# A two-layer decoder trunk: the sums of the adaLN modulation, from Pool during the attention to VectorE during the input projection

## The chip, the core and the metric

The kernel runs on one core of one Trainium2 chip. The metric is the time of one execution on the device in microseconds, the median over runs. The engines are named as in the profile: PE is TensorE's matmul, PEld its weight load, DVE is VectorE, ACT is ScalarE, POOL is GpSimd ("Pool" here), and SP is the engine that issues most DMAs.

## What is computed

Two layers over 512 tokens of 1024 columns, in float32. Each layer is an attention sub-layer of four groups of heads behind one input projection, and a sub-layer of experts. Both are modulated by six vectors that come from the condition `c`:

```
for l in range(DEPTH):
    mod = jax.nn.silu(c) @ ada_w[l] + ada_b[l]
    sh1, sc1, g1, sh2, sc2, g2 = [m[:, None, :] for m in jnp.split(mod, 6, axis=-1)]
    h = rms_norm(x, norm_mix_g[l]) * (1.0 + sc1) + sh1
    x = x + g1 * hybrid_mixer(h, l, w_in[l], ...)
    h = rms_norm(x, norm_ffn_g[l]) * (1.0 + sc2) + sh2
    x = x + g2 * peer_ffn(h, peer_w_q[l], ...)
```

Each vector is a product of 1024 numbers with a 1024x1024 block of `ada_w`. The change concerns the vectors 2, 3 and 4 of each layer (`g1`, `sh2`, `sc2`). They are not needed before the output projection (`g1`) and the second norm.

## The kernel before

A vector j of the modulation is made in eight steps k. Step k loads 128 rows of its block, 128x1024 or 512 KB, as a tile `aw` (`ada_load`, L223), multiplies every row by its element of silu(c), and adds the result to a sum `aacc`. At the end TensorE adds `aacc` down its 128 partitions (`ada_sum`): for `g1` as a row in two halves (L241), for `sh2` and `sc2` as eight columns (L239). `ada_put` adds the bias; the row of `g1` goes through DRAM (`rowd`) to come back on all partitions (`grow`). The vectors 0 and 1 of layer 0 are made at the start by VectorE with one instruction for a step (`ada_mac`, L218 and L220); vector 5 and the vectors 0 and 1 of layer 1 in the same way during the experts. The vectors 2 to 4 are made during the attention, as below.

The input projection (`w_in_phase`) multiplies the normed rows with `w_in` in seven chunks of 256 to 384 columns. Rows and weights are split in a high and a low part (`hh`, `hl`; `wh`, `wl`), and three matmuls (`mm3`, L203 to L205) make a product. For each chunk four quarters of the weights are loaded (`wr`, two slots), copied by ScalarE to `wh` (L598) and subtracted by VectorE to `wl` (L599); there are six slots of `wh` and `wl`, so the first two quarters of the next chunk can be made early and the other two once the last tile of tokens of this chunk has read its first rows. Then come four tiles of 128 tokens, each with 24 matmuls, whose result VectorE rotates (`rope`, L346 to L348, with its sum on Pool, L349) or ScalarE copies. Behind a chunk stands the making ready of heads (`behind`): Pool or VectorE copies a head twice side by side (`two`, L494), and TensorE transposes it (L497). In layer 0 chunk 0 runs in an order written by hand while the tiles of rows are still normed: `norm_parts` makes `hf` (L318, L320), and `put_split` makes `hh` and `hl` from it (L338, L339). Elsewhere in the projection a scheduler orders the instructions. In layer 1 chunk 0 is done by the end of layer 0.

The attention runs in an order from a planner (`Plan`). Each piece of work has a due time and an engine with a rough length; pieces start when inputs, buffers and engine allow, the most urgent first. Pieces may name several engines. `W` is VectorE working on tiles in SBUF alone and `G` is Pool, and the planner lets both hold a common thing called `port`, so that in its plan they are never at work at once. Its pieces: scores (L851), their maximum (L860), exponentials on ScalarE (L865), the sums' reciprocals, the weights (L874 on ScalarE, L876 on VectorE; for the differential heads L1072, L1077, L1079, L1084), transposes (L884), copies out of PSUM (L790, L792) and sums of values. At the end of the list stands the modulation: loads on SP, a multiplication on Pool or, for each third, on ScalarE (`ada_times`, L273 and L275), and a sum on Pool (L1340), with two buffers `aw` and two `aacc` of the attention's room.

`O`, 128 x 8 x 512, holds the attention's output until the output projection. In layer 0 the input rows lie in it first, a tile of tokens in two of its eight parts; nothing else uses it before the attention.

Of the kernel before, what the change touches and what calls it, by code (L numbers as in the profile page):

```python
# [55 lines left out]
# the chunks of w_in: for each run of columns the size of the rotated heads, the tile, the place in it, the width  # L56
# [7 lines left out]
SV = 0.0  # L64
# [35 lines left out]
class Plan:  # L100
    """an order for pieces of work, from rough lengths: each starts as soon as its inputs, buffers and engine allow, the most urgent first"""
# [28 lines left out]
    def holds(self, eng):  # L130
        """what a piece of work holds: its engine, and the way to SBUF that vector operations on two tiles (W) share with Pool"""
# [20 lines left out]
def trunk(ctx: ExitStack, tc: tile.TileContext, I, out):  # L152
# [81 lines left out]
    def ada_sum(j, acc, c):  # L234
        """sums over the rows, down the partitions or along the free axis"""
# [35 lines left out]
    def ada_times(eng, d, w, k):  # L271
        if eng is S:
            S.activation(d, w, AF.Copy, scale=sil[:, k:k + 1])  # L273
        else:
            eng.tensor_mul(d, w, bc(sil[:, k:k + 1], [128, D]))  # L275

    def norm_cols(l, which):
        """the scale and the shift of a norm, once they are asked for"""
# [13 lines left out]
    def norm_parts(x, cols, pool, put, tag, nv=NV):  # L292
        """normed and modulated rows of one token tile, transposed, four chunks at a time: four steps"""
# [68 lines left out]
    def rows_out(l):  # L362
        """what is done with each tile of rows that leaves layer l - 1"""
        if l == L:
# [19 lines left out]
            def halves(i, x, pool):  # L384
                """the same for a tile of rows that comes in two halves"""
# [28 lines left out]
    def early_mc(nat_):  # L414
        """the place of the first chunk's columns until the tiles they lie in are needed"""
# [3 lines left out]
    def first_chunk(nat_, hh, hl):  # L419
        """the products with the first chunk of w_in, for a tile of rows and some of the inner blocks"""  # L420
# [12 lines left out]
    class Room:  # L433
        """a pool over parts of tiles that nothing else needs yet"""
# [8 lines left out]
    def begin(O, RST, tp, more, hh, hl):  # L443
        """the modulation of the first norm, and what is done around the first chunk of w_in"""
# [39 lines left out]
    def w_in_phase(l, raw_, hh, hl, tp, pa, RST, O):  # L484
        """the products with w_in; what the heads need is made ready behind the chunk that follows"""
# [1659 lines left out]
```

## Time and profile before

| | us |
|---|---|
| three runs | 3385.28, 3389.96, 3396.86 |
| median | 3389.96 |
| span of the profiled execution | 3387.4 |
| median less that span | 2.6 |
| PE, DVE, ACT, POOL busy | 3202.0, 2593.0, 1542.2, 988.0 |

The profile is of one execution, and the page gives its span from the first to the last instruction. The median of the runs is 2.6 us longer, so what is worked out against the span is moved by that much. Layer 0 takes the first half: the projection runs to 161.3, the attention to 334.5, and the output projection and the experts follow; layer 1's projection ends at 1832 and its attention at 2007.3. Busy times overlap: PE's share of 95% of the whole span is a mean over stages, and the attention is one where it is lower.

### The profile page before, as it was taken

The numbers are of one execution on the slowest core, as the hardware profiler recorded it, in microseconds if no ns is written. First come the engines' busy times: TensorE is split into PE (matmuls) and PEld (weight loads), VectorE is DVE, ScalarE is ACT, GpSimd is POOL, SyncE is SP. The second block draws the span as 40 slices with busy tenths as digits, with TensorE's granted clock in tenths as the row PEclk, the third lists the DMA queues.
The fourth block names the chain that finished last, engine by engine and source line by source line (L and its number), as shares of the span: only waits on it lengthen the run. The fifth ranks groups of instructions, "written<-read, shape, count | busy, mean of one in ns | idle before, by whom it ended". The sixth has DMA issues, their size and how long they took to land.

```text
span 3387.4 us, 48323 instructions
## 1 busy us (share of the span) xinstructions
PE 3202.0 (95%) x17540; PEld 2820.4 (83%) x17540; DVE 2593.0 (77%) x5460; ACT 1542.2 (46%) x2799; POOL 988.0 (29%) x756
## 2 busy tenths in 40 slices
PE   6988999979999999999999889999799999999998
PEld 6955879968989999998898568798699899999987
DVE  6487699867878888786665877988587788777766
ACT  3376526883333333333344764278633333333333
POOL 1254120003434343341023532100143344444400
PEclk9988999979999999999998999998799999999999
DMA  6223404458989998896632233044588899999954
GB/s 219 66 92 101 158 26 144 174 210 313 346 308 339 337 335 328 326 351 231 200 117 74 90 125 139 28 154 180 221 320 326 315 341 325 324 324 325 323 186 166
DMA packets 291342, 762.76 MB, mean 225 GB/s; under 512 B 23832, under 2 KB 130968, under 8 KB 285984
## 3 DMA queue, kind: packets, MB, share of 16 engines
q1 hardware_dynamic: 217376, 491.22, 42.0%
q0 software_dynamic: 73728, 268.47, 21.5%
q8 instruction: 137, 2.24, 0.3%
q14 instruction: 101, 0.83, 0.1%
HBM read 700.86 MB, written 58.74 MB: 224 GB/s over the span
## 4 chain that ended last, share of the span: by engine, by line
PE 76%; DVE 13%; ACT 6%; DMA 2%; issue 1%; POOL 0%; SPq 0%; DVEq 0%; POOLq 0%; ACTq 0%
PE psa L204 13%; PE psa L205 13%; PE psa L203 13%; PE psb L203 9%; PE psb L205 9%; PE psb L204 9%; ACT gs L1689 3%; PE psa L1683 2%; PE psa L851 2%; ACT og L1673 2%; DMA gq<-gdram 1%; PE psa L884 1%; DVE s L1466 1%; DVE ki L1464 1%; DVE ki L1470 1%
## 5 line engine op out<-in xcount | busy, mean ns | idle before, releaser
L203 PE MATMUL psb<-bh,uh 128*128 128x384 f32 x2048 | 692.0, 338 | 3.4 <-ACT act L1392 2.8
L205 PE MATMUL psb<-bh,ul 128*128 128x384 f32 x2048 | 688.7, 336 | 3.1 <-DVE ul L1379 3.1
L204 PE MATMUL psb<-bl,uh 128*128 128x384 f32 x2048 | 687.2, 336 | 0.0
L203 PE MATMUL psa<-vh,wdh 128*128 128x512 f32 x1512 | 590.3, 390 | 17.2 <-ACT wdh L1844 17.2
L205 PE MATMUL psa<-vh,wdl 128*128 128x512 f32 x1512 | 593.5, 393 | 0.0
L204 PE MATMUL psa<-vl,wdh 128*128 128x512 f32 x1512 | 593.3, 392 | 0.0
L1779 POOL DMA_INDIRECT gt<-in_peer_u,eid x256 | 338.2, 1321 | 727.9 <-DVE gt L1799 234.8
L1844 ACT ACTIVATE wdh<-act 128x384 fp32r<-128x384 f32 x252 | 132.1, 524 | 866.2 <-PE psa L204 637.3
L1779 POOL DMA_INDIRECT gt<-in_peer_v,eid x256 | 323.0, 1262 | 426.5 <-DVE a L1804 197.9
L203 PEld LDWEIGHTS psb<-bh,uh 128*128 128x128 f32 x2048 | 386.4, 189 | 13.8 <-ACT act L1392 4.0
L204 PEld LDWEIGHTS psb<-bl,uh 128*128 128x128 f32 x2048 | 385.9, 188 | 7.3
L205 PEld LDWEIGHTS psb<-bh,ul 128*128 128x128 f32 x2048 | 385.3, 188 | 4.8 <-DVE ul L1379 4.4
L1379 DVE TENSOR_TENSOR ul<-ur,uh 128x1024 fp32r<-128x1024 f32 x246 | 301.6, 1226 | 98.4 <-ACT uh L1376 84.9
L1845 DVE TENSOR_TENSOR wdl<-act,wdh 128x384 fp32r<-128x384 f32 x252 | 140.9, 559 | 285.4 <-ACT wdh L1844 274.5
L203 PEld LDWEIGHTS psa<-vh,wdh 128*128 128x128 f32 x1512 | 285.0, 189 | 73.0 <-ACT wdh L1844 17.8
L205 PEld LDWEIGHTS psa<-vh,wdl 128*128 128x128 f32 x1512 | 284.8, 188 | 60.0
L1856 DVE TENSOR_TENSOR vl<-vr,vh 128x1024 fp32r<-128x1024 f32 x252 | 307.7, 1221 | 34.1 <-ACT vh L1853 22.8
L204 PEld LDWEIGHTS psa<-vl,wdh 128*128 128x128 f32 x1512 | 284.8, 188 | 55.8
L1804 DVE SCALAR_TENSOR_TENSOR a<-gt,w,a 128x1024 f32<-128x1024 f32 x254 | 325.5, 1282 | 0.8
L1799 DVE SCALAR_TENSOR_TENSOR gt<-gt,h 128x1024 f32<-128x1024 f32 x256 | 310.8, 1220 | 0.0
L1376 ACT ACTIVATE uh<-ur 128x1024 fp32r<-128x1024 f32 x256 | 268.5, 1049 | 75.4 <-PE psb L204 63.6
L1392 ACT ACTIVATE act<-psb 128x384 f32<-128x384 f32 x256 | 126.8, 495 | 334.6 <-PE psb L205 334.5
(386 smaller groups left out, 5565.5 us busy)
## 6 DMA issues: line engine op xcount, KB each, us to landing
ur<-in_peer_uT SPq DMA_DIRECT2D x256, 512.0 KB
vr<-in_peer_v SPq DMA_DIRECT2D x256, 512.0 KB
gdram<-gs SPq DMA_DIRECT2D x24, 2048.0 KB
gq<-gdram SPq DMA_DIRECT2D x64, 768.0 KB
aw<-in_ada_w SPq DMA_DIRECT2D x58, 512.0 KB
gt<-in_ada_w SPq DMA_DIRECT2D x32, 512.0 KB
wr<-in_w_q SPq DMA_DIRECT2D x14, 1024.0 KB
wr<-in_w_out SPq DMA_DIRECT2D x16, 512.0 KB
```

What stands on the lines that cost most here:

```text
L203: PE.matmul(ps, lhsT=wh, rhs=mh, start=first, stop=False)
L204: PE.matmul(ps, lhsT=wh, rhs=ml, start=False, stop=False)
L205: PE.matmul(ps, lhsT=wl, rhs=mh, start=False, stop=last)
L1376: S.activation(uspl[e][0], uraw[e], AF.Copy)
L1379: eng.tensor_sub(uspl[e][1], uraw.pop(e), uspl[e][0])
L1392: S.activation(acts[e], ups.pop(e)[:, :384], AF.Gelu_apprx_tanh)
L1779: G.indirect_dma_start(out=t, out_offset=None, in_=I["peer_u" if kind == "u" else "peer_v"], in_offset=bass.IndirectOffsetOnAxis(ap=eid3[: ...
L1799: V.scalar_tensor_tensor(t, t, 1.0, h3, op0=ALU.mult, op1=ALU.mult, accum_out=d3[:, s:s + 1])
L1804: V.scalar_tensor_tensor(a3, t, w3[:, s:s + 1], a3, op0=ALU.mult, op1=ALU.add)
L1844: S.activation(wh, w, AF.Copy)
L1845: V.tensor_sub(wl, w, wh)
L1856: V.tensor_sub(vspl[e][1], vraw.pop(e), vspl[e][0])
```

## The change

The planner's pieces for the modulation are taken out, together with `ada_times` and the buffers `aw` and `aacc` of the attention. In their place `more_ada(ch)` is called after each of the chunks 1 to 6 of the input projection, for four steps each: load, `ada_mac` on VectorE, and after the eighth step of a vector `ada_finish`. The tiles lie in `O`: two slots for `aw` in its first four parts and two for the sums in the last four; the row of `g1` lies in the first row of `h3`. The scheduler is free to move these instructions among those of the chunks.

```
+            flat = [O[:, 2 * i:2 * i + 2].rearrange("p a t -> p (a t)") for i in range(NT)]
+            room = Room(aw=flat[:2], aacc=flat[2:], arow=[h3[0:1]])
+            acc = {}
+
+            def more_ada(ch):
+                for n in range(4 * (ch - 1), 4 * ch):
+                    j, k = 2 + n // KD, n % KD
+                    if k == 0:
+                        acc[j] = room.tile([128, D], F32, name="aacc", tag="aacc", bufs=2)
+                    aw = room.tile([128, D], F32, name="aw", tag="aw", bufs=2)
+                    ada_load(l, j, k, aw)
+                    ada_mac(acc[j], aw, k)
+                    if k == KD - 1:
+                        ada_finish(l, j, acc[j], room.tile([1, D], F32, name="arow", tag="arow", bufs=1) if j == 2 else None)
...
                 for f in behind.get(ch, ()):
                     f()
+                if ch > 0:
+                    more_ada(ch)
...
-    plan = Plan({"a": 6, "b": 2, "P": PB[0], "PT": PB[1], "grp": NGRP, "pc": 2, "th": 2, "mu": 2, "aw": 2, "aacc": 2, "wo": 2}, AT0, SV)
+    plan = Plan({"a": 6, "b": 2, "P": PB[0], "PT": PB[1], "grp": NGRP, "pc": 2, "th": 2, "mu": 2, "wo": 2}, AT0, SV)
...
-    prev, t0, dt = None, 3.0, clock[0] / 27
-    for j in range(2, 5):
-        for k in range(KD):
-            a = plan.add(t0, lambda j=j, k=k: step_load(j, k), ("Q", 1.8), take=("aw",), after=merge([prev]))
-            prev = a
-            m = plan.add(t0 + 2, lambda e, j=j, k=k: step_times(j, k, e), [("G", 1.9)] if (8 * j + k) % AM else [("S", 1.05)], after=[a], take=("aacc",) if k == 0 else (),
-                         give=(("aw", a),) if k == 0 else ())
-            if k == 0:
-                t, m0 = m, m
-            else:
-                t = plan.add(t0 + 4, lambda j=j, k=k: G.tensor_add(acc[j], acc[j], tw[j, k]), ("G", 2.3), after=[m, t], give=(("aw", a),))
-            t0 += dt
...
```

Pool's row in layer 0, from the last rotations of the projection (`dk`) on; `aacc` and `aw` are the modulation's, `qC` and `qD` tiles of the differential heads. Before:

```order
L349 TENSOR_TENSOR dk<-dk,rt_1287 128x256
L349 TENSOR_TENSOR dk<-dk,rt_1317 128x256
L1169 MEMSET qC 128x2048
L275 TENSOR_TENSOR aacc<-aw,sil 128x1024
L275 TENSOR_TENSOR aw<-aw,sil 128x1024
L1340 TENSOR_TENSOR aacc<-aacc,aw 128x1024 x2
L275 TENSOR_TENSOR aw<-aw,sil 128x1024
L1340 TENSOR_TENSOR aacc<-aacc,aw 128x1024
L275 TENSOR_TENSOR aw<-aw,sil 128x1024
L1340 TENSOR_TENSOR aacc<-aacc,aw 128x1024 x2
```

and now, down to the powers of the two head norms (`drs`) and of the second norm (`nrs`):

```order
L343 TENSOR_TENSOR dk<-dk,rt_1337 128x256
L343 TENSOR_TENSOR dk<-dk,rt_1367 128x256
L1181 MEMSET qC 128x2048
L1181 MEMSET qD 128x2048
L1156 TENSOR_TENSOR drs<-dms,nhalf 128x8 x2
L200 TENSOR_TENSOR nrs<-rsq,nhalf 128x1 x4
```

Nothing of the modulation is left in Pool's row. VectorE's row in layer 0, at the end of chunk 0: the last two halves of tile 1 and the first of tile 2 become `hf`, `hh` and `hl`; `mc` are columns of chunk 0 that are normed for later. Before:

```order
L320 TENSOR_SCALAR hf0_119<-psa_331,ngs_221,mcol_127 128x128
L338 CAST hh_91<-hf0_119 128x4x128
L339 TENSOR_TENSOR hl_92<-hf0_119,hh_91 128x4x128
L199 TENSOR_SCALAR rsq_587<-css_582 128x1
L199 TENSOR_SCALAR rsq_590<-css_582 128x1
L525 TENSOR_SCALAR mc_110<-mc_110,crs_583 128x256
L526 TENSOR_SCALAR mc_110<-mc_110,crs_583 128x128
L320 TENSOR_SCALAR hf0_119<-psa_362,ngs_221,mcol_127 128x128
L338 CAST hh_91<-hf0_119 128x4x128
L339 TENSOR_TENSOR hl_92<-hf0_119,hh_91 128x4x128
```

and now, with the modulation's steps as instructions on `O`:

```order
L314 TENSOR_SCALAR hf0_119<-psa_331,ngs_221,mcol_127 128x128
L199 TENSOR_SCALAR rsq_587<-css_582 128x1
L199 TENSOR_SCALAR rsq_590<-css_582 128x1
L332 CAST hh_91<-hf0_119 128x4x128
L519 TENSOR_SCALAR mc_110<-mc_110,crs_583 128x256
L333 TENSOR_TENSOR hl_92<-hf0_119,hh_91 128x4x128
L520 TENSOR_SCALAR mc_110<-mc_110,crs_583 128x128
L220 SCALAR_TENSOR_TENSOR O_99<-O_99,sil_73 128x1024
L314 TENSOR_SCALAR hf0_119<-psa_362,ngs_221,mcol_127 128x128
L220 SCALAR_TENSOR_TENSOR O_99<-O_99,sil_73 128x1024
L332 CAST hh_91<-hf0_119 128x4x128
L333 TENSOR_TENSOR hl_92<-hf0_119,hh_91 128x4x128
```

Two multiply-adds stand around the second of these `hf`, and a first product and a multiply-add stand shortly ahead of these rows; before, neither place has any. SP's row in layer 0, from the first weights of chunk 1 (`wr`) on, with `wk` and the small tiles for later. Before:

```order
L593 DMA wr_437<-in_w_in 128x2x320
L593 DMA wr_443<-in_w_in 128x2x320
L516 DMA mg_116<-in_mla_g 128x3
L552 DMA wk_114<-in_wk 64x2048
L553 DMA wk_114<-in_wv 64x2048
L593 DMA wr_449<-in_w_in 128x2x320
L593 DMA wr_455<-in_w_in 128x2x320
L554 DMA posk_115<-in_pos 128x32
L798 DMA lamv_1575<-in_lam 128x128
L808 DMA subg_1584<-in_sub_g 128x1
L811 DMA sink_1587<-in_sinks 128x4
L280 DMA ng_3355<-in_norm_g 128x8
```

and now:

```order
L603 DMA wr_437<-in_w_in 128x2x320
L603 DMA wr_443<-in_w_in 128x2x320
L510 DMA mg_116<-in_mla_g 128x3
L223 DMA O_99<-in_ada_w 128x1024 x2
L256 DMA h3_84<-in_ada_b 1x1024
L603 DMA wr_449<-in_w_in 128x2x320
L603 DMA wr_455<-in_w_in 128x2x320
L223 DMA O_99<-in_ada_w 128x1024 x2
L546 DMA wk_114<-in_wk 64x2048
L223 DMA O_99<-in_ada_w 128x1024 x2
L547 DMA wk_114<-in_wv 64x2048
L603 DMA wr_642<-in_w_in 128x768
```

The loads of `ada_w` into `O` stand between those of `w_in`, and the ones of `wk` further back. In the planner's row of VectorE in the attention, which has no place here, the weights that VectorE takes rise from 46 to 68 (L876) and from 4 to 18 (L1079) over both layers, and the copies out of PSUM that it takes fall from 68 to 52.

## Rows read from the trace of the kernel before

**Rows 1.** Busy time by stretch: projection and attention of layer 0, then layer 1.
```profile
core 0: us, PE busy (x) PEld busy (x) DVE busy (x) ACT busy (x) POOL busy (x), PEclk, DMA share, GB/s
60.00:161.30 101.30, 101.28 (x768) 99.31 (x767) 47.48 (x112) 28.06 (x55) 28.48 (x40) 1.00 0.24 68
161.30:334.50 173.20, 143.83 (x841) 93.24 (x841) 138.74 (x386) 121.12 (x334) 88.35 (x41) 0.88 0.31 99
1735.00:1832.00 97.00, 96.99 (x738) 95.13 (x737) 46.99 (x103) 26.72 (x47) 26.35 (x36) 1.00 0.27 76
1832.00:2007.30 175.30, 145.18 (x849) 95.11 (x846) 139.61 (x386) 121.68 (x335) 88.54 (x41) 0.87 0.31 97
```

**Rows 2.** Waits of PE, layer 0's attention (us, times, longest): first and last of twelve.
```profile
PE psa L884 <- DVE P L1084: 10.7, 5, 3.8
...
PE psa L884 <- DVE mq L348: 0.2, 1, 0.2
```

**Rows 3.** Chain of waits, layer 0's attention: start, us, what.
```profile
168.15 1.71 DVE rzc L1010
...
217.21 0.95 PE psb L241 x2
...
268.18 1.69 PE psb L239 x16
...
302.31 2.10 DVE co L1072
...
327.06 1.68 PE psb L239 x16
```

**Rows 4.** Two lines in layer 0's attention: shortest, median and longest in ns.
```profile
L1072 DVE TENSOR_SCALAR co<-rz,lam x8: 229/428/2103, 251.2 to 302.3; 128x4 f32<-128x4 f32 x8
...
L916 DVE TENSOR_TENSOR esink<-nm,nsink x4: 155/162/2035, 218.4 to 240.5; 128x4 f32<-128x4 f32 x4
```

**Rows 5.** Timelines of DVE and of POOL from 229 to 232 us: start, us.
```profile
229.49 2.04 DVE L916 TENSOR_TENSOR esink<-nm,nsink 128x4 f32<-128x4 f32 x1
...
229.15 2.36 POOL L1340 TENSOR_TENSOR aacc<-aacc,aw 128x1024 f32<-128x1024 f32 x1
```

**Rows 6.** Instructions on the tile aw in layer 0's attention: shortest, median, longest in ns.
```profile
L1340 POOL TENSOR_TENSOR aacc<-aacc,aw x21: 2343/2361/2490, 171.8 to 319.8; 128x1024 f32<-128x1024 f32 x21
L275 POOL TENSOR_TENSOR aw<-aw,sil x14: 1887/1902/2871, 169.8 to 299.0; 128x1024 f32<-128x1024 f32 x14
L273 ACT ACTIVATE aw<-aw,sil x7: 1134/1137/1149, 181.2 to 318.5; 128x1024 f32<-128x1024 f32 x7
```

**Rows 7.** The same tile's name in the first 40 us, where VectorE makes the steps.
```profile
L220 DVE SCALAR_TENSOR_TENSOR aacc<-aw,sil,aacc x9: 745/1285/1285, 9.8 to 29.6; 128x1024 f32<-128x1024 f32 x7, 128x512 f32<-128x512 f32 x2
L218 DVE TENSOR_SCALAR aacc<-aw,sil x2: 749/751/753, 8.5 to 20.3; 128x1024 f32<-128x1024 f32 x2
```

**Rows 8.** Timelines of DVE and PE at the last tile of chunk 0, layer 0.
```profile
53.34 0.43 DVE L338 CAST hh<-hf 128x512 fp32r<-128x512 f32 x1
53.80 0.69 DVE L339 TENSOR_TENSOR hl<-hf,hh 128x512 fp32r<-128x512 f32 x1
...
54.84 0.34 PE L203 MATMUL psa<-wh,hh 128*128 128x384 f32 x1
...
55.19 0.34 PE L205 MATMUL psa<-wh,hl 128*128 128x384 f32 x1
```

**Rows 9.** Waits in layer 0's projection, 60 to 161.3 us.
```profile
ACT wh L598 <- PE psa L205: 29.7, 6, 8.8
```

**Rows 10.** Timelines of POOL and of DVE from 135 to 138 us, in chunk 6.
```profile
135.91 2.28 POOL L349 TENSOR_TENSOR dk<-dk,rt 128x256 f32<-128x256 f32 x1 [2.50 <-DVE dk L348]
...
135.76 1.87 DVE L565 TENSOR_TENSOR x<-x,posk 128x992 f32<-128x992 f32 x1
```

**Rows 11.** Instructions on the tile two in layer 0's projection, 60 to 161.3 us.
```profile
L494 POOL COPY two<-rq x4: 610/612/617, 75.4 to 91.2; 128x512 f32<-128x512 f32 x4
L494 POOL COPY two<-rk x4: 610/616/1080, 109.0 to 122.6; 128x512 f32<-128x512 f32 x4
```

More of the change, by code (lines that the diff above doesn't have):

```diff
@@ L269, in grow @@
         return m[j]
-    def ada_times(eng, d, w, k):
-        if eng is S:
-            S.activation(d, w, AF.Copy, scale=sil[:, k:k + 1])
-        else:
-            eng.tensor_mul(d, w, bc(sil[:, k:k + 1], [128, D]))
     def norm_cols(l, which):
@@ L665, in trunk @@
                 (ocm, op, w0), split_w_out = attention(nc, tc, I, l, lam_init, st, O, RST, tp, small, bank, rope, nhalf, ca, ident, cst["blk"],
-                                                   rcm, right, (ada_load, ada_times, ada_sum, ada_put, ada_row))
+                                                   rcm, right)
             hcm, hpool = right(tc.tile_pool(name=f"hB{l}", bufs=1))
@@ L774, in attention @@
 @with_exitstack
-def attention(ctx, nc, tc, I, l, lam_init, st, O, RST, tp, small, bank, rope, nhalf, ca, ident, blk, rcm, right, ada):
+def attention(ctx, nc, tc, I, l, lam_init, st, O, RST, tp, small, bank, rope, nhalf, ca, ident, blk, rcm, right):
     V, S, G, PE, SY = nc.vector, nc.scalar, nc.gpsimd, nc.tensor, nc.sync
@@ L1308, in attention @@
         g.keep_plan(4, 2, t, g.first)
-    load, times, total, put, row = ada
-    acc, tw = {}, {}
-    def step_load(j, k):
-        tw[j, k] = at.tile([128, D], F32, name="aw", tag="aw", bufs=2)
-        load(l, j, k, tw[j, k])
-    def step_times(j, k, eng):
-        if k == 0:
-            acc[j] = at.tile([128, D], F32, name="aacc", tag="aacc", bufs=2)
-        times(E[eng], acc[j] if k == 0 else tw[j, k], tw[j, k], k)
-    def step_row(j):
-        tw[j] = at.tile([1, D], F32, name="arow", tag="aw", bufs=2)
-        row(l, j, tw[j])
-    def step_sum(j, c):
-        tw[j, "s", c] = total(j, acc[j], c)
-    prev, t0, dt = None, 3.0, clock[0] / 27
-    for j in range(2, 5):
-        for k in range(KD):
-            a = plan.add(t0, lambda j=j, k=k: step_load(j, k), ("Q", 1.8), take=("aw",), after=merge([prev]))
-            prev = a
-            m = plan.add(t0 + 2, lambda e, j=j, k=k: step_times(j, k, e), [("G", 1.9)] if (8 * j + k) % AM else [("S", 1.05)], after=[a], take=("aacc",) if k == 0 else (),
-                         give=(("aw", a),) if k == 0 else ())
-            if k == 0:
-                t, m0 = m, m
-            else:
-                t = plan.add(t0 + 4, lambda j=j, k=k: G.tensor_add(acc[j], acc[j], tw[j, k]), ("G", 2.3), after=[m, t], give=(("aw", a),))
-            t0 += dt
-        s = None
-        if j == 2:
-            r = prev = plan.add(t0, lambda j=j: step_row(j), ("Q", 0.5), take=("aw",), after=[prev])
-        for c in range(2 if j == 2 else 1):
-            end = c == (1 if j == 2 else 0)
-            s = plan.add(t0 + 6, lambda j=j, c=c: step_sum(j, c), ("PE", 0.9 if j == 2 else 1.5), after=merge([t, s]), take=("b",),
-                         give=(("aacc", m0),) if end else ())
-            t = plan.add(t0 + 8, lambda j=j, c=c: put(l, j, tw[j, "s", c], c, tw.get(j)), ("V", 0.7 if j == 2 else 0.2), after=merge([s, r if j == 2 else None, t]),
-                         give=(("b", s),) + ((("aw", r),) if j == 2 and end else ()))
     with tc.manual_schedule():
```

## The prediction

> **What bounds the kernel now.** I read the busy time by stretch first. In both layers the input projection runs with TensorE full (101.28 of 101.30 us, and 96.99 of 97.00) while VectorE is half idle, and the attention behind it runs with no engine full: in layer 0, of 173.2 us, TensorE 143.8, VectorE 138.7, ScalarE 121.1, Pool 88.4, at a mean granted clock of 0.88; in layer 1, of 175.3 us, almost the same [rows 1]. So work that goes from the attention to the projection leaves a stretch where TensorE waits for others and enters one where VectorE has room but TensorE has none.
>
> Next, who makes TensorE wait in the attention. Its waits add up to 28.9 us in twelve groups, and 27.5 of these end with a VectorE instruction [rows 2]; that agrees with the 29.4 us for which the first view leaves TensorE idle. So VectorE is what ends last. Then the chain of waits, in the same stretch: between 168.15 and 302.31 it has 21 pieces of VectorE that look wrong for their size, such as 2.10 us for an instruction on 128x4 elements [rows 3]. That same instruction takes 0.23 us at its shortest and 2.10 at its longest; another on 128x4 takes 0.155 and 2.035 [rows 4]. Lay the longest of these beside Pool's timeline: it starts at 229.49, Pool's sum starts at 229.15 and ends at 231.51, and VectorE's instruction ends at 231.53, 0.02 later [rows 5]. All 21 pieces lie against a multiplication or a sum of the modulation on Pool in this way. They take 39.8 us; at the shortest duration that each of their instructions has in the stretch they would take 7.3. So some 32 us of layer 0's chain is VectorE standing behind Pool. Over all of VectorE's instructions there the surplus is 43.9 us, and 44.0 in layer 1.
>
> What a page says of this comes behind the row: the Trainium skill, SBUF — State Buffer, section Who interferes with whom, says that Pool and VectorE share one pair of ports, that a VectorE instruction with two SBUF inputs, or in a two-port mode, needs it against a Pool instruction that reads SBUF, and that whoever comes second stands until the first is through. The trace agrees: the stalls end with Pool's instruction.
>
> **The change part by part.** *Removed from the attention.* Per layer 16 multiplications at 1.9 us and 21 sums at 2.36 us on Pool, about 80 us of its 88, and 8 multiplications at 1.14 us on ScalarE [rows 6] (the rows show those that write `aw`; the first of each vector writes `aacc`). Pool keeps two fills and two small powers, so nearly all of the 32 us of stalls goes. Also TensorE's products of the sums: two halves of a row at 0.95 us each and two columns at 1.69, together 5.3 us, all four pieces on the chain [rows 3].
>
> What the attention gets from this has two bounds. By the chain it is 32 + 5.3 = 37 us, if no other path stands behind the one shortened. From below it is the 5.3 us alone, if every stall only hid another wait. Between them stands TensorE: without the sums it has 138.5 us of work at the clock that it had, so with no idle time at all it could save 34.7. Some idle time stays, at the start, where the first scores must be exponentiated before anything can be transposed, and in the turns between tiles. I take two thirds of the 29.4 idle us, 19.6, and the 5.3: **25 us a layer**. It is nearer to the upper end because 27.5 of 28.9 us of TensorE's waiting is for VectorE, and VectorE's 138.7 us fall to about 95 when 43.9 go. The order also changes here: without Pool's pieces, which the planner let hold the same way to SBUF as VectorE's, it gives VectorE more of the weights and ScalarE more of the copies out of PSUM; VectorE can carry that with 95 of 173 us.
>
> *Added to the projection.* Per layer 3 first products at 0.75 us and 21 multiply-adds at 1.285, 29.2 us of VectorE [rows 7]. In layer 0 VectorE has 47.5 busy us in the 101.3 of chunks 1 to 6, in layer 1 47.0 in 97 [rows 1], so there is room; what it costs is where one stands ahead of something TensorE is about to read. I followed the order of after through the trace's times.
>
> - Layer 0, last tile of chunk 0. Before, its first `hh` and `hl` are ready at 53.77 and 54.49, and TensorE takes them at 54.84 and 55.19 [rows 8]: 1.1 and 0.7 us of slack. The new order puts four steps of the modulation ahead of that `hh`, 0.75 + 3 x 1.285 = 4.6 us, while some 1.2 us of VectorE's idle time and 1.2 of small instructions for later lie there to be taken up. So `hh` comes about 3.5 us later than before, at 57.3: 2.5 us late. It is the first tile of the kernel's projection, TensorE has nothing else, and **2.5 us** it costs; without the 2.4 us that I counted as taken up it would be near 5.
> - Later chunks. The weights' low parts `wl` of the third and fourth quarter can only be made once the last tile of the chunk before has read its first rows (ScalarE's wait for that is 29.7 us in six) [rows 9], and they are needed some 5/16 of a chunk later, 4.7 us of the 15 or so that a chunk takes. Ahead of them the new order has at most two multiply-adds, 2.6 us, and a tile's rotation, 1.1. That fits, so I count nothing; if it does not, each chunk costs up to 1.5 us, 9 a layer.
> - The queue. On SP each of the 24 loads, 512 KB, stands between the loads of `w_in` and waits until its slot's multiply-add is through; loads of `wr` queue behind it. These run one chunk ahead and the 16 DMA engines are 0.24 busy there [rows 1]; hidden, unless VectorE falls behind first.
> - Pool and VectorE can stand behind each other here as well, since Pool makes the rotations' sums and some copies. Where such a pair meets now, VectorE's sum on 128x992 and Pool's `dk` start within 0.15 us, and Pool's takes 2.28 us [rows 10]. Behind Pool's copies `two` (0.61 us, eight a layer) [rows 11] stand TensorE's transposes. I take **1 us a layer**, since these copies are few and the order leaves about 2 us of products between them; the worst is 8 x 1.285 = 10 us a layer.
> - TensorE's 5.3 us of sums now stand in a stretch where it is full: **5.3 us a layer**.
>
> The sum: gained 2 x 25 = 50; paid 2 x 5.3 + 2.5 + 2 x 1 = 15. The span of 3387.4 us falls by 35 to 3352.4. The runs' median is 2.6 us over that span, which gives **3355 us**. What follows the attention is moved as a whole: the output projection starts when the attention's room is free.
>
> **The rivals.**
> - *The stalls go along in full.* Each of Pool's eight copies `two` in a projection waits for a whole multiply-add, and TensorE for the copy: 10 us a layer in place of 1, 3355 + 18 = 3373. For it speaks the pair at 135.76 [rows 10]; against it, that Pool only has 28.5 busy us of 101.3 there [rows 1]. Chance 0.08. The page's rule above (the Trainium skill, SBUF — State Buffer, Who interferes with whom) makes no difference between the two stretches: a multiply-add reads two tiles in SBUF, and so do Pool's sums.
> - *Another wait takes the place.* TensorE's waits move from VectorE to ScalarE, which has 121 - 9 = 112 us of its own, and the attention gains 10 us a layer: 3387.4 - 20 + 15 + 2.6 = 3385. Against it: ScalarE ends only about 1.4 us of TensorE's waits now. Chance 0.12.
> - *VectorE becomes the bound of the projection.* One mechanism, in the chunks of layer 0 and 1: a multiply-add waits at the head of VectorE's queue for its 512 KB load, since only two slots turn, and the `wl` behind it comes late. Net nothing is left when this costs 17.5 us a layer beyond what I counted, 0.7 us for each of the 24; at 1.285 for each, 31 us, the time is 3355 + 62 = 3417. Against it: the order spreads the 24 of layer 0 over what were 48 to 125 us, 3.2 us for each, so that a slot has some 6 us for its load and its multiply-add. Chance 0.08, slower.
> - *The clock comes along.* A mean of 0.88 says that TensorE stood at the lower of its levels, 1.2 GHz for 2.4, in about 0.24 of the attention, 41 us [rows 1]. If it was busy there as in the mean, 34 us of work would take 17 at the upper level. With fewer gaps some of it comes back: an attention shorter by 35 to 40, 3325 to 3335. Chance 0.12.
>
> **How the numbers follow.** My forecast, a gain of 17 to 32 us an attention against 13 to 22 paid, spans 3339 to 3378 and has 0.60. With the clock's case below and most of the case where another wait takes over above, 8 in 10 lie in 3325 to 3384. What the measurement can tell from no change is about 0.3%, 10 us. Faster by more than that (below 3380): 0.60 + 0.08 + 0.12 = 0.80; the same: 0.12; slower: 0.08.
>
> **What would show it.** The attention of each layer, from the first scores to the last sums of values, falls from 173 and 175 to about 148 and 150 us; L1072's and L916's instructions of before lose their 2 us cases, and VectorE's busy time there falls below 105; Pool's is under 10. The projection of layer 0 grows by some 9 us, of layer 1 by 6, with TensorE full but for about 2.5 us at the end of chunk 0. I am wrong if TensorE shows waits for `wl` or `two` in the projection of more than some 10 us a layer, or if its waits in the attention stay near 29 us with other names.

## Result and the profile after

The changed kernel takes 3339.63 us (median of 4 runs, 3335.71 to 3348.45), the kernel before 3392.47 beside it. The ratio is 0.9858, its 95% interval 0.9836 to 0.9881: faster, by 1.4%. A later series of the same file, `after_again` below, gave 3341.33 and 0.9859 (0.9844 to 0.9874). The profiled execution's span falls from 3387.4 to 3339.8 us, by 47.6.

Busy time by stretch of the changed kernel comes first, in the columns of [rows 1]: the projection of layer 0 from chunk 1's first products to the convolution's first, the attention from there to the output projection's first product, and the same of layer 1. These marks are instructions, so they are not the round times of [rows 1]: the convolution's first product in layer 0 stands at 152.73 before, where that view ends the projection at 161.3.

```profile
64.73:171.60 106.87, 99.38 (x658) 95.95 (x657) 76.52 (x138) 28.56 (x54) 40.12 (x40) 0.97 0.52 156
171.60:311.97 140.37, 133.94 (x955) 93.04 (x954) 102.69 (x397) 109.60 (x321) 6.95 (x4) 0.98 0.09 28
1707.00:1819.75 112.75, 102.47 (x662) 97.43 (x661) 82.59 (x140) 29.66 (x55) 41.23 (x41) 0.97 0.63 195
1819.75:1960.31 140.56, 134.40 (x955) 93.67 (x954) 102.61 (x397) 109.64 (x321) 6.95 (x4) 0.96 0.09 28
```

The same stretches, marked by the same instructions, in the kernel before:

```profile
59.03:152.73 93.70, 93.68 (x642) 92.35 (x641) 47.69 (x110) 28.05 (x53) 28.48 (x40) 1.00 0.26 73
152.73:335.26 182.53, 152.40 (x974) 101.16 (x973) 139.39 (x390) 122.63 (x339) 88.35 (x41) 0.89 0.30 94
1728.63:1823.87 95.24, 94.04 (x641) 92.25 (x640) 49.81 (x113) 29.32 (x55) 29.00 (x41) 1.00 0.32 92
1823.87:2007.81 183.94, 153.31 (x975) 102.69 (x974) 140.25 (x390) 122.93 (x339) 88.54 (x41) 0.88 0.30 93
```

The attentions get 42.2 and 43.4 us shorter, 85.5 together. Layer 0's convolution starts 18.9 us later (171.60 for 152.73) and layer 1's projection takes 17.5 more, 36.4 together. That leaves some 49 of gain, and the span shows 47.6. VectorE's busy time in an attention falls from 139 to 103 us, Pool's from 88 to 7, and TensorE's granted clock rises from 0.89 to 0.98 in layer 0 and from 0.88 to 0.96 in layer 1.

The instructions of [rows 4], now at lines 1084 and 928, have lost their long cases (ns, shortest, median, longest):

```profile
L1084 DVE TENSOR_SCALAR co<-rz,lam x8: 229/230/231, 250.2 to 283.9; 128x4 f32<-128x4 f32 x8
...
L928 DVE TENSOR_TENSOR esink<-nm,nsink x4: 154/158/164, 228.4 to 242.0; 128x4 f32<-128x4 f32 x4
```

TensorE's waits in layer 0's attention, 28.9 us in [rows 2], are the five below from 180 us to just ahead of the output projection, and add up to 5.1:

```profile
PE psa L863 <- DVE nm L872: 1.3, 2, 0.8
PE psa L896 <- ACT P L886: 1.2, 2, 0.8
PE psa L1185 <- DVE nm L872: 1.2, 1, 1.2
PE psa L896 <- DVE P L888: 1.0, 2, 0.6
PE psa L1150 <- ACT sn L1146: 0.4, 1, 0.4
```

In the projections, where TensorE waited for 0.0 and 1.2 us before, its waits are now 7.5 us in layer 0 (the first two lines, and 0.2) and 10.2 in layer 1 (the other four, and three under 1 us):

```profile
PE psb L491 <- DVE nq L494: 5.6, 1, 5.6
PE psb L491 <- DVE sq L494: 1.7, 1, 1.7
```

```profile
PE psb L491 <- POOL dq L343: 3.5, 1, 3.5
PE psa L203 <- ACT wh L608: 2.7, 2, 2.5
PE psa L204 <- DVE wl L609: 1.7, 3, 1.1
PE psb L491 <- DVE nq L494: 1.1, 1, 1.1
```

L491 are the transposes of the heads (L497 before). So the longest wait of each layer is ahead of a transpose, not for weights (`wh`, `wl`).

### The profile page after: what moved, and what is told of

The parts are those of the page before. It is cut to its first block, busy times and chain, and to the rows that moved or that the text cites. A ratio compares the mean times of both kernels' runs of the same rounds, so it can differ in the third digit from the quotient of the medians.

```text
span 3339.8 us, 48260 instructions
## 1 busy us (share of the span) xinstructions
PE 3183.5 (95%) x17540; PEld 2816.0 (84%) x17540; DVE 2585.4 (77%) x5528; ACT 1516.9 (45%) x2763; POOL 851.9 (26%) x682
## 4 chain that ended last, share of the span: by engine, by line
PE 75%; DVE 11%; ACT 8%; DMA 4%; issue 2%; POOL 0%; SPq 0%; DVEq 0%; ACTq 0%; POOLq 0%
PE psa L204 12%; PE psa L205 12%; PE psa L203 12%; PE psb L203 10%; PE psb L205 9%; PE psb L204 9%; ACT gs L1660 3%; PE psa L1654 2%; ACT og L1644 2%; PE psa L863 2%; PE psa L896 1%; DMA gq<-gdram 1%; DVE s L1437 1%; DMA wr<-in_w_in 1%; ACT P L877 1%
## 5 line engine op out<-in xcount | busy, mean ns | idle before, releaser
L1815 ACT ACTIVATE wdh<-act 128x384 fp32r<-128x384 f32 x252 | 132.1, 524 | 862.2 <-PE psa L204 640.6
L203 PEld LDWEIGHTS psb<-bh,uh 128*128 128x128 f32 x2048 | 386.6, 189 | 13.2 <-DVE arow L250 2.6
```

Source lines behind the costliest of these rows:

```text
L203: PE.matmul(ps, lhsT=wh, rhs=mh, start=first, stop=False)
L1815: S.activation(wh, w, AF.Copy)
```

## Experiments

All times are medians beside runs of the kernel before on the same chip; stretches are those of the tables above. One caution: the second profile of the changed kernel shows the convolution at 175.1 us where the first shows 171.6, and 108.8 us for layer 1's projection where the first shows 112.8. A projection is thus known to some 4 us; the attentions agree within 0.01.

The theory is that of the prediction: in the attention VectorE stood behind Pool. The rivals: the planner's new order made the gain, or the change of place did.

### Pool alone: taken from before, given to after

`pool_gone` is before without Pool's 21 sums and 14 of its 16 multiplications a layer (the first products stay), but with its order:

```
-        times(E[eng], acc[j] if k == 0 else tw[j, k], tw[j, k], k)
+        if k == 0 or eng == "S":
+            times(E[eng], acc[j] if k == 0 else tw[j, k], tw[j, k], k)
...
-                t = plan.add(t0 + 4, lambda j=j, k=k: G.tensor_add(acc[j], acc[j], tw[j, k]), ("G", 2.3), after=[m, t], give=(("aw", a),))
+                t = plan.add(t0 + 4, lambda: None, ("G", 2.3), after=[m, t], give=(("aw", a),))
```

> The kernel before, with Pool's pieces of the modulation planned but not issued: 14 of the 16 multiplications a layer and all 21 sums are left out (the modulation vectors are wrong), the two first products on Pool, ScalarE's 8 multiplications, the 24 loads and TensorE's products of the sums stay, and every other engine has its instructions in exactly the order of before. Theory (VectorE stands behind Pool in the attention): the attention of each layer, 182.5 and 183.9 us from the convolution's first product to the output projection's first, falls by 32 to 38 us to some 148, with the granted clock going from 0.89 to 0.96 or more; the whole time falls by 65 to 75 us to 3317 to 3327. Rival (the planner's new order, with more of the weights on VectorE, and the work taken from ScalarE made the gain): the attention falls by under 10 us a layer, the time stays above 3370.

`pool_back` is after with Pool's work on tiles of zeros (a loop over 24 steps):

```
...
+        if n % AM:
+            t = plan.add(t0, lambda: G.tensor_mul(dw, dw, bc(ident[:, 0:1], [128, D])), ("g", 1.9), after=merge([t]))
+        if n % KD:
+            t = plan.add(t0 + 2, lambda: G.tensor_add(da, da, dw), ("g", 2.3), after=merge([t]))
...
```

> The changed kernel, with Pool alone given back what it did in the attention: 16 multiplications and 21 sums a layer on two tiles of zeros that nobody else reads, spread over the same span of the plan, without loads, without sums on TensorE; the order on the other four engines is that of the changed kernel, instruction for instruction. Theory (stalls): the attention goes from 140.4 back up by 30 to 40 us a layer, its granted clock back to about 0.90, the time to 3400 to 3420, slower than before. Rival (order and ScalarE's relief): the attention stays under 150, the time under 3360.

Measured: without Pool's pieces 3332.21 us, ratio 0.9831 (0.9814 to 0.9849), attentions of 157.0 and 150.8 at a clock of 0.91 and 0.97. They are 25.5 and 33.1 us shorter, so layer 0 and the time miss the theory's 32 to 38 and 3317 to 3327, while the rival's bounds (under 10, above 3370) are far off. With the pieces put back 3419.95, ratio 1.01 (1.008 to 1.0121), slower than before and at the upper end of the theory's range, attentions of 180.65 and 180.93:

```profile
173.24:353.89 180.65, 152.39 (x955) 101.20 (x954) 147.63 (x397) 110.22 (x321) 89.13 (x43) 0.85 0.07 22
```

Against layer 0's attention of the changed kernel, the 955 matmuls and 397 VectorE instructions are the same, in the same order. VectorE is busy 44.9 us longer for them, TensorE loses clock (0.85 for 0.98) and 40.3 us are gone. Pool's pieces were to be spread over the attention, but on the chip they stand between 183.8 and 279.1 us. That gives a comparison within the run: cut behind them (290 us), and in the changed kernel ahead of the same last 411 matmuls (248 us), the first part takes 116.76 us for 76.40, the rest 63.89 for 63.97. First with Pool back, then the changed kernel:

```profile
173.24:290.00 116.76, 92.29 (x546) 62.13 (x546) 98.10 (x220) 55.48 (x165) 85.79 (x41) 0.77 0.02 7
290.00:353.89 63.89, 60.10 (x411) 39.07 (x410) 49.53 (x178) 54.74 (x157) 3.34 (x2) 1.00 0.16 50
```

```profile
171.60:248.00 76.40, 73.76 (x545) 53.89 (x545) 53.06 (x220) 54.80 (x165) 3.61 (x2) 0.96 0.03 10
248.00:311.97 63.97, 60.19 (x411) 39.15 (x411) 49.62 (x179) 54.80 (x157) 3.34 (x2) 1.00 0.16 50
```

All that is lost is lost while Pool works. Groups by line show which instructions get longer, first with Pool back, then in the changed kernel (count, busy us, mean ns):

```profile
L872 DVE CUSTOM_DVE_ANT_0 P<-psa,consts_a 128x512 f32<-128x512 f32 x20 | 13.5, 686 | 1.4 <-PE psa L863 1.2
...
L983 DVE TENSOR_TENSOR rz<-rz,gate 128x4 f32<-128x4 f32 x8 | 11.0, 1381 | 0.3
...
L888 DVE TENSOR_SCALAR P<-P,rz 128x512 f32<-128x512 f32 x9 | 10.8, 1227 | 0.1
...
L881 DVE RECIPROCAL rz<-Z 128x4 f32<-128x4 f32 x24 | 4.1, 171 | 1.0 <-ACT P L877 0.8
```

```profile
L872 DVE CUSTOM_DVE_ANT_0 P<-psa,consts_a 128x512 f32<-128x512 f32 x20 | 13.4, 687 | 1.2 <-PE psa L863 1.0
...
L881 DVE RECIPROCAL rz<-Z 128x4 f32<-128x4 f32 x24 | 4.2, 174 | 1.5 <-ACT P L877 1.2
L888 DVE TENSOR_SCALAR P<-P,rz 128x512 f32<-128x512 f32 x9 | 4.1, 484 | 0.1
...
L983 DVE TENSOR_TENSOR rz<-rz,gate 128x4 f32<-128x4 f32 x8 | 1.3, 164 | 0.3
```

The product of two SBUF tiles (L983) goes from 164 to 1381 ns and the scaling from SBUF to SBUF (L888) from 484 to 1227, while the reciprocal and the instruction that has only one input in SBUF, the other in PSUM (L872), do not change. The timelines of VectorE and Pool with Pool back show one case: VectorE's 128x4 ends at 192.56, Pool's sum at 192.54.

```profile
190.99 1.57 DVE L983 TENSOR_TENSOR rz<-rz,gate 128x4 f32<-128x4 f32 x1
```

```profile
190.19 2.35 POOL L1330 TENSOR_TENSOR da<-da,dw 128x1024 f32<-128x1024 f32 x1
```

The Trainium skill, SBUF — State Buffer, Who interferes with whom, counts among the instructions that meet Pool those with two SBUF inputs, copies and `tensor_scalar` in a two-port mode, and exempts others with at most one SBUF input. The trace agrees with these 1381 and 1227 for the first and 171 and 686 ns for the second (that L888 runs in such a mode no row says).

So Pool's presence costs 40 us an attention in the new order, where its pieces stand close together, and 25 to 33 in the old one, where they stand between 167.9 and 322.1 us. The rival (order alone) is out.

### The rest of the attention's gain

`all_gone` is before's order with none of the modulation issued (the loads are left out likewise):

```
...
-        times(E[eng], acc[j] if k == 0 else tw[j, k], tw[j, k], k)
+        return
...
-        tw[j, "s", c] = total(j, acc[j], c)
+        tw[j, "s", c] = None
```

> The kernel before with all pieces of the modulation in the attention planned but not issued: Pool's multiplications and sums, ScalarE's eight multiplications, the 24 loads and TensorE's products of the sums are left out (the modulation vectors are the biases alone), VectorE's small additions stay as copies; every engine's other instructions stand in the order of before. The kernel with Pool's pieces alone gone has attentions of 157.0 and 150.8 us, the changed kernel 140.4 and 140.6. If that rest is the sums, ScalarE's multiplications, the loads and the clock that they cost, both attentions come to 139 to 143 us and the time to 3296 to 3306. If it is the order that the planner makes without those pieces, they stay at 146 us or more and the time above 3310.

Measured: 3316.94 us, 0.9791 (0.9768 to 0.9815), attentions of 149.05 and 144.23. The first theory's 139 to 143 is missed in both layers, and the second's bound of 146 is kept only in layer 0; the time lies above 3310, as the second has it. Of layer 0's 42.2 us, 25.5 go with Pool's pieces, 8.0 with the sums, ScalarE's pieces and loads, and 8.7 are what the planner's new order adds; in layer 1 33.1, 6.6 and 3.7. The two layers have the same instructions in the same order; they differ in clock, 0.93 and 0.98:

```profile
153.01:302.06 149.05, 138.62 (x939) 93.64 (x938) 103.46 (x390) 113.47 (x331) 7.16 (x4) 0.93 0.09 30
1791.21:1935.44 144.23, 133.09 (x939) 90.47 (x938) 103.27 (x390) 113.11 (x331) 7.16 (x4) 0.98 0.10 31
```

### Engine or place

`dve_attn` is before with the modulation left in the attention and put on VectorE (`times` is `ada_mac` there):

```
-        times(E[eng], acc[j] if k == 0 else tw[j, k], tw[j, k], k)
+        times(acc[j], tw[j, k], k)
...
-            m = plan.add(t0 + 2, lambda e, j=j, k=k: step_times(j, k, e), [("G", 1.9)] if (8 * j + k) % AM else [("S", 1.05)], after=[a], take=("aacc",) if k == 0 else (),
+            m = plan.add(t0 + 2, lambda e, j=j, k=k: step_times(j, k, e), [("W", 1.285 if k else 0.75)], after=merge([a, t if k else None]), take=("aacc",) if k == 0 else (),
...
-                t = plan.add(t0 + 4, lambda j=j, k=k: G.tensor_add(acc[j], acc[j], tw[j, k]), ("G", 2.3), after=[m, t], give=(("aw", a),))
+                t = m
```

> The kernel before, complete, with the modulation left in the attention, but as 3 products and 21 multiply-adds a layer on VectorE, planned there, in place of Pool's and ScalarE's pieces: the engine is changed and the place is not. Theory (VectorE behind Pool was the cost; 29 us of its own work fit in the attention's slack): attentions of 152 to 162 us, projections as before, the time 3330 to 3350, about that of the changed kernel. Rival (the place is what matters, VectorE is the bound of the attention with 29 us more): attentions of 170 us or more, the time 3362 or more.

Measured: 3331.53 us, 0.9827 (0.9806 to 0.9848), attentions of 153.22 and 154.90, projections as before (93.56 and 95.54). These are the theory's numbers: the attentions gain less than with the move (29 us each for 42 and 43), the projections pay nothing, and the whole gains as much. The move itself was not needed for the gain.

```profile
152.40:305.62 153.22, 140.84 (x974) 94.53 (x973) 125.01 (x415) 115.63 (x330) 7.89 (x4) 0.97 0.35 112
```

VectorE is busy 125 of 153 us here, 14 less than with Pool beside it, though it does 24 steps more.

### What the projection pays

`no_steps` leaves out 21 loads and 21 multiply-adds a layer:

```
-                    ada_load(l, j, k, aw)
-                    ada_mac(acc[j], aw, k)
+                    if k == 0:
+                        ada_load(l, j, k, aw)
+                        ada_mac(acc[j], aw, k)
```

> The changed kernel with 21 of the 24 steps a layer left out (the loads and the multiply-adds; the three first products, their loads and TensorE's sums stay; the modulation vectors are wrong). Theory (the steps on VectorE and what they wait for cost the projection beyond the 5.3 us of sums): the projection of layer 0 ends 12 to 14 us earlier, that of layer 1 10 to 12, the attention stays at 140, the time is 3313 to 3318. Rival (the sums and the clock that a stretch behind them loses cost it): under 4 us a layer, 3332 to 3340.

`one_load` leaves out 21 loads a layer alone:

```
-                    aw = room.tile([128, D], F32, name="aw", tag="aw", bufs=2)
-                    ada_load(l, j, k, aw)
+                    if k == 0:
+                        aw = acc["w"] = room.tile([128, D], F32, name="aw", tag="aw", bufs=2)
+                        ada_load(l, j, k, aw)
+                    aw = acc["w"]
```

> The changed kernel with one load for each vector in place of eight: all 24 products and multiply-adds stay on VectorE, but 21 of the 24 loads of 512 KB are left out, so that no multiply-add but the first of a vector waits for a transfer (the modulation vectors are wrong). Theory 1 (VectorE waits at the head of its queue for loads, and the weights' low parts and rotations behind stand): it gets back two thirds or more of what the kernel without steps gets back, 16 to 25 us in all. Theory 2 (the multiply-adds themselves, Pool and VectorE behind each other, and the late first tile cost it): under a third, 0 to 8 us.

`loads_only` leaves out 21 multiply-adds a layer alone:

```
-                    ada_mac(acc[j], aw, k)
+                    if k == 0:
+                        ada_mac(acc[j], aw, k)
```

> The changed kernel with all 24 loads a layer but only the three first products: 21 multiply-adds are left out (the modulation vectors are wrong). With neither loads nor multiply-adds layer 0's convolution starts at 159.1 us and layer 1's projection takes 103.0; with the multiply-adds alone 166.4 and 101.9. If the transfers themselves cost (they crowd out the weights of the chunks), layer 1's projection is 107 us or longer and the time 3326 to 3336. If loads cost only because multiply-adds stand and wait for them at the head of VectorE's queue, both stay within 3 us of the kernel with neither, the time is 3317 to 3324.

Measured: 3319.77 us (0.9804, 0.9787 to 0.982), 3322.55 (0.9809, 0.9793 to 0.9825) and 3326.08 (0.9817, 0.9794 to 0.984). In layer 0 the convolution starts at 159.1 with neither, 165.3 with loads alone, 166.4 with multiply-adds alone, 171.6 with both: each costs some 6 or 7 us, beside the 6.3 that remain with neither (3.4 of them TensorE's sums). In layer 1 the projection takes 103.0, 101.6, 101.9 and 112.75: there neither costs anything alone and both together cost 6 to 10. With one profile of each and 4 us of uncertainty, the times are the firmer measure: against 3319.77 with neither, multiply-adds alone cost 2.8 us, loads alone 6.3 and both 21.6 (3341.33); by the ratios 2, 4 and 19. So most of the cost needs both.

For the theories this means: `no_steps` lies within its theory's range in layer 0 (12.5 us) and just outside it in layer 1 (9.8) and in the time. `one_load` gives back 19 of the 21.6 us, as its first theory said; but `loads_only` gives back 15 of the same 21.6, so such a share does not tell the cause. In `loads_only` the crowded transfers are not the cause in layer 1 (101.6, not 107), and its other theory (within 3 us of the kernel with neither) fails in layer 0, by 6.2 us.

What loads and multiply-adds do together shows in part in the waits of layer 1's projection (us, times, longest). ScalarE's wait for the chunks' weights is 16.3 us with neither, 23.2 with multiply-adds, 32.9 with loads, and in the changed kernel

```profile
ACT wh L608 <- DMA wr<-in_w_in: 57.6, 18, 9.8
```

and SP, which issues both kinds of loads in one order, stands there at the modulation's loads until a multiply-add has freed their slot:

```profile
SPq L223 <- DVE O L220: 30.6, 18, 5.8
```

With multiply-adds alone that wait is 6.2 us, with loads alone none (3.3 behind the first products). The second profile of the changed kernel has 38.6 and 28.2 in these two rows, and its projection is shorter by 4 us: TensorE's wait of 2.47 us for `wh` at 1727.82, with a clock of 0.57 in the 4 us behind it, is 0.5 there. That SP's standing makes the weights late fits all of these; it was not tried with a queue of its own for the loads. And it is a part only: TensorE's direct waits for `wh` and `wl` are 4.4 of 10.2 us in layer 1 (2.3 of 7.7 in the second profile) and none in layer 0.

In layer 0, VectorE's own waits for these loads are larger, 8.9 us from 40 us on against 4.6 in layer 1's projection. Its timeline shows a pair, the second waiting 2.09 us for its load, and what leads from there to TensorE's longest wait:

```profile
92.22 1.28 DVE L220 SCALAR_TENSOR_TENSOR O<-O,sil 128x1024 f32<-128x1024 f32 x1 [1.13 <-DMA O<-in_ada_w]
95.60 1.29 DVE L220 SCALAR_TENSOR_TENSOR O<-O,sil 128x1024 f32<-128x1024 f32 x1 [2.09 <-DMA O<-in_ada_w]
...
97.80 2.40 DVE L609 TENSOR_TENSOR wl<-wr,wh 128x664 fp32r<-128x664 f32 x2
100.12 1.62 DVE L220 SCALAR_TENSOR_TENSOR O<-O,sil 128x1024 f32<-128x1024 f32 x1
...
102.78 1.30 DVE L494 TENSOR_TENSOR nq<-psb,nq 64x512 fp32r<-64x512 f32 x2
```

```profile
103.62 1.09 PE L491 MATMUL psb<-consts,two 128*128 128x128 f32 x4 [5.62 <-DVE nq L494]
```

The transposes write to a bank (`psb`) that ScalarE and VectorE must first have read for `nq`. ScalarE was done at 96.7, but VectorE came to it at 102.78, behind the late multiply-add, two `wl`, another multiply-add and two rotations. Pool is in it too: a pair of its copies `two` takes 2.78 us from 99.44 on, where one took 0.61 before [rows 11]. In the 4 us behind this wait the granted clock is 0.58. The wait is 5.8 us in the second profile, 3.9 with multiply-adds alone and 3.0 in `rope_v` below, where Pool has no rotation's sum; the shares of queue and Pool were not separated. With loads alone one of 4.6 us stands there, ahead of a sum (L241), behind ScalarE: it had stood 4.96 us at `wh` for late weights, and `nq` came behind them.

At the end of chunk 0, the `hh` and the product that [rows 8] have at 53.34 and 54.84 stand as follows, on VectorE's timeline and then TensorE's:

```profile
56.70 1.29 DVE L220 SCALAR_TENSOR_TENSOR O<-O,sil 128x1024 f32<-128x1024 f32 x1 [1.44 <-DMA O<-in_ada_w]
57.90 0.42 DVE L332 CAST hh<-hf 128x512 fp32r<-128x512 f32 x1
```

```profile
58.47 0.41 PE L203 MATMUL psa<-wh,hh 128*128 128x384 f32 x1 [2.06 <-DVE hh L332]
```

The first `hh` is 4.6 us later, the product 3.6, and chunk 1 starts 5.7 us later (64.73 for 59.03). The rest lies behind the product, at a lower granted clock; from there to chunk 1, before and now:

```profile
54.84:59.03 4.19, 4.19 (x25) 4.19 (x25) 2.87 (x14) 2.76 (x8) 1.09 (x2) 1.00 0.01 2
```

```profile
58.47:64.73 6.26, 6.26 (x28) 6.26 (x28) 5.40 (x12) 1.48 (x2) 1.24 (x2) 0.73 0.88 205
```

### Other places, and Pool out of the projection

`paced` queues each step on VectorE behind a rotation (`more_ada` takes the next steps there, and its calls behind the chunks go):

```
...
-                            rope(dst, ps[:, c:c + m], m // kind, kind, cc[:, i], ss[:, i], wp)
+                            r = rope(dst, ps[:, c:c + m], m // kind, kind, cc[:, i], ss[:, i], wp)
+                            with tc.issue_after(r.ins):
+                                more_ada(2 if at == 3 and ch < 5 else 1)
```

> The changed kernel, complete, with each step of the modulation queued on VectorE right behind the rotation of one tile of rows: one step behind each rotation of chunks 1 to 5, a second one behind the last rotation of chunks 1 to 4, so none in chunk 0 and none in chunk 6. Slots, loads and arithmetic are those of the changed kernel. Theory (the steps come too early and in pairs: they stand ahead of the first tile in chunk 0, and a pair waits for its two loads): layer 0's convolution starts at 160 to 164 us in place of 171.6, layer 1's projection takes 103 to 107 in place of 112.75, VectorE waits for those loads under 2 us a layer, the time is 3316 to 3328. Rival (the multiply-adds cost what they cost wherever they stand, by Pool and VectorE behind each other): the projection is shorter by under 4 us a layer, the time is 3332 or more.

`paced_late` keeps chunk 1 free as well (against `paced`):

```
...
-                            with tc.issue_after(r.ins):
-                                more_ada(2 if at == 3 and ch < 5 else 1)
+                            if ch > 1:
+                              with tc.issue_after(r.ins):
+                                    more_ada(2 if at % 2 == 0 else 1)
```

> The changed kernel, complete, with the steps behind the rotations of chunks 2 to 5 alone (two behind the first and third tile, one behind the second and fourth), so that chunk 1's weights, the constants and the convolution's weights are loaded first. Theory (crowded transfers at the projection's start cost layer 1 what pacing won): from the first transposes of layer 1 to its output projection 278 to 282 us in place of 286 in the paced kernel, the time 3318 to 3327. Rival (24 steps in four chunks keep VectorE and the transfers too busy): the same as the paced kernel or longer, 3328 to 3342.

`rope_v` moves the rotations' sums, `paced_nopool` these and the copies `two` of queries in the paced kernel:

```
...
-        eng.tensor_add(dst, dst, t)
+        (eng or V).tensor_add(dst, dst, t)
...
-            (V if key else G).tensor_copy(two, bc(src[:, :, None, :], [128, NT, 2, 64]))
+            if key:
+                V.tensor_copy(two, bc(src[:, :, None, :], [128, NT, 2, 64]))
+            else:
+                S.activation(two, bc(src[:, :, None, :], [128, NT, 2, 64]), AF.Copy)
```

> The changed kernel, complete, with the rotations' sums (20 a layer in the projection) on VectorE in place of Pool: some 0.45 us each more on VectorE, 9 us a layer, and Pool left with copies. Theory (Pool and VectorE behind each other cost most of the projection's 17 to 19 us): multiply-adds on 128x1024 fall to 1.3 us each, the projections get shorter by 5 us or more each, the time is 3320 to 3330. Rival (loads and places cost it): the projections change by under 3 us each, or get longer, the time is 3334 to 3350.

> The changed kernel, complete, with the steps queued behind the rotations as in the kernel with paced steps, the rotations' sums on VectorE, and the eight copies of queries to be transposed on ScalarE in place of Pool. If both the places and Pool count, it is faster than each alone: projections of 100 to 104 us behind chunk 0, 3308 to 3320. If Pool costs nothing once the steps are paced, it equals the paced kernel within 5 us; if VectorE's 9 us more count, it is slower than that by 5 or more.

And the changed kernel once more, as their measure:

> The changed kernel itself, on the same chip as the three others: 0.984 to 0.988 of the time of the kernel before, some 3338 us. Both theories expect the same; it is the measure for the three others.

Measured: `paced` 3331.05 us (0.9836, 0.9823 to 0.985), `paced_late` 3330.37 (0.9821, 0.9803 to 0.9839), `rope_v` 3334.19 (0.9843, 0.9828 to 0.9858), `paced_nopool` 3332.49 (0.9835, 0.9821 to 0.9848), the changed kernel again 3341.33. All four are 7 to 11 us under that last one (`paced_late` was timed in another set of runs, with `dve_attn`), and their slowest run (3337.34) is under its fastest (3338.48); beside its first series (3335.71 to 3348.45) and by the ratios' intervals, which touch or overlap, this is a small gain and no large one. Chunk 0's 5.7 us do go with pacing, but none reaches its first theory's range of time, VectorE still waits 3.1 and 5.0 us for the loads in `paced`, and the projections stay long: the convolution of layer 0 at 169.4, 168.0, 168.9 and 165.5, layer 1's projection 114.3, 112.6, 111.9 and 119.9 (in the order of the times above). In the paced kernels some 1.9 us of this is the last vector's sums, which the changed kernel has behind the convolution; their attentions are 3 to 4 us shorter. So places and Pool cost a few us each, and most of layer 1's payment stays with all of them. `dve_attn`, `paced`, `paced_late` and `paced_nopool` are the fastest complete kernels here, 3330 to 3333 us, and cannot be told apart.

## Why the prediction held, and which terms were off

The forecast of 3355 us is 15 above the result; 3339.6 lies inside its own range of 3339 to 3378, at the edge. The mechanism of the gain is shown: `pool_gone` and `pool_back` take Pool's pieces away and bring them back alone. That the sum came near is luck: two terms were too small on opposite sides, the gain by 36 us over both layers and the payment by 21.

- *Attention, 25 us a layer: 42.2 and 43.4.* I took two thirds of TensorE's 29.4 idle us, 19.6, at the clock that it had. In layer 0 TensorE's idle time fell from 30.1 to 6.4 us, 23.7, so that part was nearly right. Of the sums 3.4 left the stretch (5.3 less the last vector's 1.88). The remaining 15.0 is TensorE's busy time for the same work, 147.1 less 132.1 once the sums are taken off: the clock came back from 0.89 to 0.98. The step that failed is "138.5 us of work at the clock that it had". I had this as the rival "the clock comes along", with 0.12 and 35 to 40 us; it came along, and the attention's gain was larger than that; the projections kept the time from its 3325 to 3335. VectorE's busy time fell by 33 in `pool_gone`, less than the 43.9 of surplus that I let go in full.
- *Projection, 8.8 and 6.3 us: 18.9 and 17.5.* Chunk 0's tail cost 5.7, not 2.5. My working of it did not come out: 4.6 us less the 2.4 counted as taken up is 2.2 and not 3.5, so with 1.1 us of slack I should have had 1.1. The product came 3.6 us late, since VectorE's idle time there was spent on a wait for a load (1.44), and the other 2.1 us are behind it, mostly the clock (0.73 for 1.00), which I had put at nothing. Later chunks cost 13.2 and 17.5, not 6.3 of sums and stalls: TensorE idles 7.5 us in layer 0, and 9.1 more than before in layer 1, and is busy 5.7 and 8.4 longer, for its sums and at a clock of 0.97. Two steps failed. One is "That fits, so I count nothing": I followed `wl` and `two` alone, and TensorE's longest wait, 5.6 us in layer 0, is for a bank that VectorE's `nq` frees, behind two multiply-adds. The other is the queue, "hidden, unless VectorE falls behind first": I had read 0.24 of the transfers' capacity and no order of events on SP, and the 3.2 us that each step had on average hid pairs of steps on two slots. For late weights TensorE waits 4.4 us in layer 1 and nothing in layer 0.
- *Port stalls in the projection, 1 us a layer.* Too small, though its size stays open. TensorE's waits ahead of the transposes, where I looked for them, are 7.3 and 5.7 us, but the queue's delays are in them. `rope_v` takes Pool's sums away, adds VectorE's, and nets 7 us of the time against the series beside it, some 3 of them in the two projections.
- *The rivals.* Another wait in TensorE's way did not come (5.1 us left). VectorE did not become the bound of the projection (76.5 of 106.9 us busy), but the mechanism of that rival, a multiply-add that waits for its load ahead of what TensorE needs, is a part of what was paid: 10 to 11 us a layer beyond my count, where it set 17.5 as the point from which nothing is left. My sign of being wrong, more than some 10 us of waits for `wl` or `two` in a projection, did not come (7.3 and 7.4).

What stays open: why loads and multiply-adds together cost layer 1 what neither does alone is argued from waits, not shown by a run; and why layer 0's attention had the lower clock in `pool_gone` and `all_gone`.

## What to carry to other kernels

Before work is moved from Pool to another stretch, try it on VectorE where it stands: Pool's 80 us cost VectorE 33 (`pool_gone`) to 45 (`pool_back`) of busy time, the same steps on VectorE cost 29 and gain as much of the whole time as the move did, with nothing paid elsewhere. When a stretch has idle TensorE time, price its gain with the clock of the full stretch as well, since here both came back together. When long steps and their loads join queues that also serve the bound engine, follow everything that engine waits for, the banks that others must free for it too, and not only the share of capacity left.

## What the hardware showed unexpectedly

- A product on 128x4 that takes 164 ns took 1381 on the mean beside Pool, longer than a scaling on 128x512 (1227). Its longest, 2233, is near the 2.36 us of one of Pool's sums: such an instruction ends with Pool's, whatever its own size.
- The same 974 or 975 matmuls of one order took 145.9 busy us in layer 0's attention and 138.2 in layer 1's (`pool_gone`), at 0.91 and 0.97 of the clock.
- Pool is held up as well: its 40 instructions in layer 0's projection took 28.5 us before and 40.1 beside the multiply-adds. In layer 1 they took 29.7 with the loads alone and 49.8 with the multiply-adds alone.
